# Attention with two heads on halves of the PE array, and full-array gated linear attention, in a transformer kernel

## The chip, the cores and the metric

The kernel runs on one core of one Trainium2 chip. The metric is the device time of one execution in microseconds (us); of several runs the median is given. TensorE (PE) is a 128x128 array: a stationary operand of K rows and M columns is loaded into it (a weight load, PEld), and a moving operand of N columns streams past. The other engines are VectorE (DVE), ScalarE (ACT), GpSimd (POOL) and SyncE (SP, which issues most transfers).

## The reference, cut to what matters

Two blocks of two layers each, batch 1, 256 latent tokens (and 256 context tokens in the first block), width 1024, all in f32. The change touches the attention of the first block's layers and the second block's last mixer. The other stages (adaptive norms, gated feed-forwards, a convolution over tokens, a state-space and mLSTM mixer, convolutional feed-forwards) are unchanged.

```python
def gqa_attention(q, k, v):                    # 6 query heads of 64, 2 key heads
    s = jnp.einsum('bqhgd,bkhd->bhgqk', qi, k).astype(jnp.float32) * scale
    p = jax.nn.softmax(s, axis=-1).astype(v.dtype)
    return jnp.einsum('bhgqk,bkhd->bqhgd', p, v)
...
# neighbourhood_attention: 6 heads; biased scores on the window, plain ones on the context
    p = jax.nn.softmax(s, axis=-1).astype(v.dtype)
    return (jnp.einsum('bhqrj,brqjhd->bqhd', p_win, vw)
            + jnp.einsum('bhqk,bkhd->bqhd', p[..., n_win:], v_ctx))
...
def _gla_scan(q, k, v, la):                    # 4 heads, key 128, value 256, chunks of 64
    bc = jnp.cumsum(la, axis=2)                # la = log_sigmoid(g_lr @ gate_w2 + gate_b) / 16
    b_end = bc[:, :, -1:]
    q_in = q * jnp.exp(bc)
    att = jnp.einsum('bclhk,bcshk->bhcls', q_in, k * jnp.exp(-bc))
    att = jnp.where(_lower_tri(l), att, 0.0)
    o = jnp.einsum('bhcls,bcshv->bclhv', att, v)
    u = jnp.einsum('bclhk,bclhv->cbhkv', k * jnp.exp(b_end - bc), v)
    # states: s_prev[c+1] = exp(b_end[c]) * s_prev[c] + u[c]
    o = o + jnp.einsum('bclhk,cbhkv->bclhv', q_in, s_prev)
```

The scan runs forward and backward over the tokens, and both results are added.

## The kernel before, in words

**Weights.** All weights stream from memory in blocks of 128x1024. SP fetches a block (`raw`), ACT copies it in the rounded type fp32r (`hi`, L115), DVE subtracts (`lo`, L116), and each weight product is three fp32r matmuls, hi·hi, hi·lo and lo·hi (`mm3` L173 to L175, `mm3t` L180 to L182). `W.to(n)` splits blocks ahead of their use. Products of f32 operands (scores times values, transposes, everything in the gated linear attention but its projections) go through the PE as plain f32; one such matmul shows as two passes in the trace, a transpose as one.

**Order.** `Builder.run` calls the stages one after the other: feed-forwards and attention of layer 0 (trace: attention about 480 to 610 us), those of layer 1 (1465 to 1578 us), the second block's mixers and feed-forwards. The gated linear attention (GLA, `mixer1`) stands at about 2256 to 2372 us. A tile framework decides the order of instructions on each engine from priorities and buffers; the kernel's generators (`fill`, `more`) only interleave independent work by hand.

**Attention (`attn`).** Keys of two heads share a 128-partition tile, 64 partitions each, keys or queries in rows and tokens in columns. There are six pairs of heads `j`; for each pair the loop goes over `nt` query tiles `t` of 128 tokens: four in layer 0 and two in layer 1 (only the latent tokens are wanted there). Tiles 0 and 1 (latent) see 512 keys, tiles 2 and 3 (context) 256. Step `i` of `6*nt + DEEP` (L914) does `scores` of its tile, and `values` of the tile two steps earlier (`DEEP` is 2). Between them `fill(n)` puts in pieces of other projections (tiles `pj`), and when those are used up, in the last layer, splits of the feed-forward's first weight blocks.

**Scores (L692).** Per head: the query's hi and lo parts lie on top of each other in the two row halves, so one matmul over K=128 against the doubled key's hi part gives two of the three products, and a second one against the key's lo part, with zeros in the other half, gives the third (L701, L702). A step has four matmuls. Then DVE adds the bias and takes the maximum, and ACT makes the exponentials `P` and their sums `sm`.

**Values (L712).** `P` is transposed on the PE in 128x128 pieces (L720), copied out of PSUM (`PT`, DVE or ACT), and each piece is the stationary operand for 64 columns of values (L729). DVE divides by the sums, and when a pair of heads is finished, its output `ot` is transposed back (`pf`, L910).

**GLA (`mixer1`).** For each of four heads and two directions (h, d): gate logits `lg` from 16 rows (L1446), cumulated and exponentiated on DVE, ACT and POOL (`gates`); then `pairs` transposes the decayed key (`kdT`, L1485) and makes the in-chunk scores `ga` (L1490). `states` multiplies 64 tokens' keys and values (`U`, L1507, K=64, rows 0 to 63 or 64 to 127 by the chunk). `outs` accumulates `go`: the in-chunk part over the whole array (L1521), then each chunk's state into 64 output columns (L1525), on the left or right half of the array by the chunk.

Of the kernel before, what the change touches and what calls it, by code (L numbers as in the profile page):

```python
# [6 lines left out]
F32 = mybir.dt.float32  # L7
# [43 lines left out]
for _name, _w in (("gf", 128), ("gbk", 128), ("rs", 256), ("w2", 512)):  # L51
    GCST[_name] = (_n, _w)
    _n += _w
# [13 lines left out]
class Weights:  # L67
# [24 lines left out]
    def _split(self, urgent=True):  # L92
        nc = self.B.nc
        b = self.split_at
        if b < self.nb:
# [3 lines left out]
            with self.B.tc.high_priority() if urgent and b >= self.B.EARLY else self.B.after_norms():  # L99
# [5 lines left out]
                for o in range(0, TPB * 128, w):  # L105
# [6 lines left out]
                    if aside and self.alone:  # L112
                        nc.gpsimd.tensor_tensor(out=hi, in0=ri, in1=self.B.zero.to_broadcast([128, w]), op=ALU.add)
                    else:
                        nc.scalar.activation(out=hi, in_=ri, func=ACTF.Copy)  # L115
                    eng.tensor_tensor(out=lo, in0=ri, in1=hi.bitcast(F32), op=ALU.subtract)  # L116
# [29 lines left out]
class Builder:  # L146
# [545 lines left out]
    def scores(self, pool, q, kz, t, bias):  # L692

        nc = self.nc
        nk, k0 = (512, 0) if t < 2 else (256, 256)
        Ps = []
        sm = self.sml.tile([128, 2], F32, tag="smx", bufs=6, name="smx")
# [12 lines left out]
        return Ps, sm, nk // 128, k0 // 128  # L710

    def values(self, pool, r, vt, vc, o):  # L712

        nc = self.nc
        r, sm, n, k0 = r
        PT = []
        for P in r:
            pt = self.psmall("pt")
            for kt in range(n):
                nc.tensor.transpose(pt[:, kt * 128:(kt + 1) * 128], P[:, kt * 128:(kt + 1) * 128], self.ident)  # L720
            x = pool.tile([128, 512], F32, tag="ck", name="PT")
            self.evac(x[:, :n * 128], pt[:, :n * 128])
            PT.append(x)
        nc.vector.reciprocal(sm, sm)
        yield
        po = self.psmall("pv")
        for a, x in enumerate(PT):
            for kt in range(n):
                nc.tensor.matmul(po[:, a * 64:a * 64 + 64], x[:, kt * 128:(kt + 1) * 128],  # L729
                                 vt[k0 + kt][:, vc + a * 64:vc + a * 64 + 64], start=kt == 0, stop=kt == n - 1)  # L730
        two = lambda x: x.rearrange("p (a b) -> p a b", a=2)
        self.tt(two(o), two(po[:, :128]), sm.unsqueeze(2).to_broadcast([128, 2, 64]), ALU.mult)

    def attn(self, l, last, end, nxt=None):
# [4 lines left out]
        if l == 0:  # L739
# [3 lines left out]

        kz = [[pool.tile([128, 512], F32R, tag="ck", name="kz") for a in range(4)]
              for i in range(3)]
        for k in kz:
            for a in range(2):
                nc.gpsimd.memset(k[2 + a][64 - 64 * a:128 - 64 * a, :].bitcast(F32), 0.0)

        def keys(k, x):  # L750
            for a in range(2):
                r, o = slice(64 * a, 64 * a + 64), slice(64 - 64 * a, 128 - 64 * a)
                self.act(k[a][r, :], x[r, :])
                self.cp(k[a][o, :], x[r, :])
                self.tt(k[2 + a][r, :], x[r, :], k[a][r, :].bitcast(F32), ALU.subtract)

        def queries(x, scale=1.0):

            q = []
            for a in range(2):  # L760
                y = pool.tile([128, 512], F32R, tag="ck", name="qs")
                r, o = slice(64 * a, 64 * a + 64), slice(64 - 64 * a, 128 - 64 * a)
                self.act(y[r, :Tq], x[r, :Tq], scale=scale)
# [1121 lines left out]
```

## Time and profile before

| | |
|---|---|
| median of 3 runs | 2582.48 us (2582.29 to 2583.18) |
| the profiled execution | 2585.52 us, of which the span of its instructions is 2583.70 us |
| PE busy | 2525.9 us, 98% of the span |
| DVE, ACT, POOL busy | 1731.0, 1193.1, 64.2 us |
| mean granted PE clock | 0.991 of full speed |
| DMA | 375.53 MB, mean 145 GB/s |

The page of the profile gives one profiled execution. A matmul's listed duration includes its way through the array, and matmuls overlap; so the price of one in a stream is the distance between the starts of neighbours, not its duration. "Waits" list the time an engine sat idle and what ended it. The granted clock is 1.00 for TensorE's upper level (2.4 GHz) and 0.50 for its lower one (1.2 GHz).

### The profile page before, as it was taken

Reading aid. Unit: us, or ns where it says so; the run is one execution under the profiler, and the core shown is the slowest. Engines: PE = TensorE matmul, PEld = TensorE weight load, DVE = VectorE, ACT = ScalarE, POOL = GpSimd, SP = SyncE. Lnnn points to the kernel's source line nnn. Section 1 sums busy time; section 2 is a strip of 40 time slices with the busy share of each in tenths; the row PEclk is TensorE's granted clock in tenths of the full one; section 3 lists DMA queues with packets and bytes.
Section 4 is the critical chain, followed back from the end, with each engine's and each line's share of the span. In section 5 each row is a group of like instructions: output and inputs, shape, how many; then the busy total and the mean of one; then the engine's idle time right before and its main releaser. Section 6 shows DMA issues by size and latency. Waiting matters only on the chain.

```text
span 2583.7 us, 37057 instructions
## 1 busy us (share of the span) xinstructions
PE 2525.9 (98%) x13876; PEld 2133.8 (83%) x13876; DVE 1731.0 (67%) x3521; ACT 1193.1 (46%) x2116; POOL 64.2 (2%) x68
## 2 busy tenths in 40 slices
PE   7999999999999999999999999999999999999999
PEld 4888888888888887888888887997988799777997
DVE  4999435665899324899324666556777787666884
ACT  4322234545422223322324555446768566566664
POOL 0000000000000000000000000000030000020000
PEclk9999999999999999999999999999999999999999
DMA  7666231212466222565222323554443355534454
GB/s 274 202 216 222 103 130 62 74 48 74 145 219 216 90 98 98 179 221 196 90 91 89 119 70 118 187 191 157 156 139 131 112 182 182 184 116 139 156 186 156
DMA packets 125028, 375.53 MB, mean 145 GB/s; under 512 B 13872, under 2 KB 15536, under 8 KB 124848
## 3 DMA queue, kind: packets, MB, share of 16 engines
q1 hardware_dynamic: 123840, 370.73, 42.3%
q8 instruction: 109, 1.79, 0.3%
q10 hardware_dynamic: 1008, 2.43, 0.3%
q14 instruction: 71, 0.58, 0.1%
HBM read 372.05 MB, written 1.05 MB: 144 GB/s over the span
## 4 chain that ended last, share of the span: by engine, by line
PE 91%; DVE 3%; ACT 3%; DMA 2%; issue 1%; POOL 0%; SPq 0%; DVEq 0%; ACTq 0%; POOLq 0%
PE pj L173 16%; PE pj L175 15%; PE pj L174 15%; PE po L180 8%; PE po L181 8%; PE po L182 8%; PE pv L729 2%; PE tm L180 2%; PE tm L182 2%; PE tm L181 2%; DMA raw<-in_w 1%; PE gp L173 1%; PE gp L174 1%; PE gp L175 1%; DVE w L116 1%; PE tr L339 1%
## 5 line engine op out<-in xcount | busy, mean ns | idle before, releaser
L115 ACT ACTIVATE w<-raw 128x1024 fp32r<-128x1024 f32 (+1 forms) x588 | 588.8, 1009 | 1002.4 <-PE pj L174 349.4
L116 DVE TENSOR_TENSOR w<-raw,w 128x1024 fp32r<-128x1024 f32 (+1 forms) x588 | 682.0, 1167 | 474.2 <-ACT w L115 470.3
L173 PE MATMUL pj<-uh,w 128*128 128x512 f32 (+1 forms) x1176 | 457.0, 389 | 2.4 <-ACT P L191 2.4
L175 PE MATMUL pj<-uh,w 128*128 128x512 f32 (+1 forms) x1176 | 455.0, 387 | 0.0
L174 PE MATMUL pj<-ul,w 128*128 128x512 f32 (+1 forms) x1176 | 454.9, 387 | 0.0
L614 DVE SCALAR_TENSOR_TENSOR aj<-adaw,cB 128x512 f32<-128x512 f32 x512 | 352.8, 689 | 8.8 <-DMA adaw<-in_wada 0.3
L173 PE MATMUL pj<-u,w 128*128 128x256 f32 x1200 | 341.5, 285 | 0.0
L175 PE MATMUL pj<-u,w 128*128 128x256 f32 x1200 | 340.0, 283 | 0.0
L174 PE MATMUL pj<-u,w 128*128 128x256 f32 x1200 | 339.8, 283 | 0.0
L180 PE MATMUL po<-w,sh 128*128 128x512 f32 x704 | 277.9, 395 | 0.0
L182 PE MATMUL po<-w,sl 128*128 128x512 f32 x704 | 276.9, 393 | 0.0
L181 PE MATMUL po<-w,sh 128*128 128x512 f32 x704 | 276.4, 393 | 0.0
L173 PEld LDWEIGHTS pj<-uh,w 128*128 128x128 f32 x1176 | 221.7, 189 | 50.9 <-ACT P L191 2.8
L175 PEld LDWEIGHTS pj<-uh,w 128*128 128x128 f32 x1176 | 221.6, 188 | 49.4 <-DVE w L116 0.3
L174 PEld LDWEIGHTS pj<-ul,w 128*128 128x128 f32 x1176 | 221.7, 189 | 47.8
L173 PEld LDWEIGHTS pj<-u,w 128*128 128x128 f32 x1200 | 229.4, 191 | 1.8 <-issue 1.3
L175 PEld LDWEIGHTS pj<-u,w 128*128 128x128 f32 x1200 | 229.7, 191 | 0.4 <-issue 0.3
L174 PEld LDWEIGHTS pj<-u,w 128*128 128x128 f32 x1200 | 229.7, 191 | 0.2
L182 PEld LDWEIGHTS po<-w,sl 128*128 128x128 f32 x704 | 132.3, 188 | 30.1
L180 PEld LDWEIGHTS po<-w,sh 128*128 128x128 f32 x704 | 132.3, 188 | 30.0 <-DVE yg L194 0.6
L181 PEld LDWEIGHTS po<-w,sh 128*128 128x128 f32 x704 | 132.3, 188 | 29.2
L194 DVE TENSOR_TENSOR sg<-sg,pj 128x512 f32<-128x512 f32 (+1 forms) x82 | 50.9, 620 | 59.1 <-PE pj L175 58.9
(380 smaller groups left out, 3588.5 us busy)
## 6 DMA issues: line engine op xcount, KB each, us to landing
raw<-in_w SPq DMA_DIRECT2D x554, 512.0 KB, 3.3
adaw<-in_wada SPq DMA_DIRECT2D x288, 256.0 KB, 3.1
bt<-in_bias SPq DMA_DIRECT2D x12, 192.0 KB, 2.4
hl<-in_x ACTq DMA_DIRECT2D x1, 512.0 KB, 5.7
hl<-in_x SPq DMA_DIRECT2D x1, 512.0 KB, 6.6
hc<-in_x SPq DMA_DIRECT2D x1, 512.0 KB, 8.6
hc<-in_x ACTq DMA_DIRECT2D x1, 512.0 KB, 8.9
gc<-in_gcst ACTq DMA_DIRECT2D x1, 512.0 KB, 3.7
```

What stands on the lines that cost most here:

```text
L115: nc.scalar.activation(out=hi, in_=ri, func=ACTF.Copy)
L116: eng.tensor_tensor(out=lo, in0=ri, in1=hi.bitcast(F32), op=ALU.subtract)
L173: mm(ps, w[0], x[0], start=first, stop=False)
L174: mm(ps, w[0], x[1], start=False, stop=False)
L175: return mm(ps, w[1], x[0], start=False, stop=last)
L180: mm(ps, x[0], w[0], start=first, stop=False)
L181: mm(ps, x[0], w[1], start=False, stop=False)
L182: mm(ps, x[1], w[0], start=False, stop=last)
L194: return self.nc.vector.tensor_tensor(out=out, in0=a, in1=b, op=op)
L339: nc.tensor.transpose(p[:, t * 128:(t + 1) * 128], hn[t][c // 4][:, (c % 4) * 128:(c % 4 + 1) * 128], self.ident)
L614: nc.vector.scalar_tensor_tensor(out=x, in0=w, scalar=1.0, in1=self.cB[:, s, i * 512:(i + 1) * 512], op0=ALU.mult, op1=ALU.mult, accum_out ...
L729: nc.tensor.matmul(po[:, a * 64:a * 64 + 64], x[:, kt * 128:(kt + 1) * 128], vt[k0 + kt][:, vc + a * 64:vc + a * 64 + 64], start=kt == 0, ...
```

## The change

**Scores.** The query and the key are each split once into hi and lo tiles of 128x512 (both heads in one instruction on ACT and one on DVE), and a step has six matmuls of K=64: three products, each for head 0 on rows 0 to 63 and head 1 on rows 64 to 127. The doubled tiles, their zeros (POOL) and the half-height copies are gone.

**Values.** Two query tiles (a pair of steps) are finished together. `P` is transposed as before, grouped by key block, always into 512-wide copies `PT`. Values are now stationary (64 columns, head 0 in columns 0 to 63 of the array, head 1 in 64 to 127), and `PT` of both tiles moves (256 columns); the output comes out with features in rows, so the transposes `pf` are gone. The inverse sums are spread by DVE to 128x256 (`rb`), transposed on the PE (2 per pair of tiles), copied by ACT, and multiplied in. A values generator yields twice, and `finish` runs once for two steps.

**Around them.** The table of exponentials is loaded ahead of the loop by a one-element activation on the last query tile. In the last layer, `fill` also runs with n=4 in the two steps behind the last scores (0 before), and from then on the copies `PT` are issued behind the newest weight split (`behind`).

**GLA.** All three small matmuls use the whole array: `lg` multiplies all rows with a table padded with zeros (2 KB wider rows of constants, 768 KB instead of 512 KB), `U` and the state part of `go` take operands padded with zeros (`kz`, `qz`; 16 memsets on POOL, and per (h, d) one ACT and one DVE copy of 64x256 and two ACT copies of 128x128 in place of one copy of 128x256). `pr_qk(3)` moves ahead of the first `pairs`.

```diff
-    def scores(self, pool, q, kz, t, bias):
+    def scores(self, pool, q, kz, t, bias, sm):
...
-        for a in range(2):
-            ps = self.psum("sc")
-            o = slice(t * 128, (t + 1) * 128)
-            nc.tensor.matmul(ps[:, :nk], q[a][:, o], kz[a][:, k0:], start=True, stop=False)
-            nc.tensor.matmul(ps[:, :nk], q[a][:, o], kz[2 + a][:, k0:], start=False, stop=True)
+        for n, (x, y) in enumerate(((0, 0), (0, 1), (1, 0))):
+            for a in range(2):
+                r = slice(64 * a, 64 * a + 64)
+                nc.tensor.matmul(pss[a][:, :nk], q[x][r, o], kz[y][r, k0:], start=n == 0, stop=n == 2)
...
+    def values(self, pool, Ps, sm, vt, vc, k0, out, behind=()):
...
+        for a in range(2):
+            for kt in range(0, n, 2):
+                pt = self.psmall("pt")
+                for k in range(2):
+                    for t in range(2):
+                        o = k * 256 + t * 128
+                        nc.tensor.transpose(pt[:, o:o + 128], Ps[t][a][:, (kt + k) * 128:(kt + k + 1) * 128],
+                                            self.ident)
+                x = pool.tile([128, 512], F32, tag="ck", name="PT")
+                with ExitStack() as es:
+                    for y in behind() if behind else ():
+                        es.enter_context(self.tc.issue_after(y.ins))
+                    self.evac(x, pt)
+                PT.append(x)
+            if a == 0:
+                r = pool.tile([128, 512], F32, tag="ck", name="rb")
+                nc.vector.reciprocal(sm, sm)
+                self.cp(r[:, :256].rearrange("p (t a n) -> p t a n", t=2, a=2), sm.unsqueeze(3).to_broadcast([128, 2, 2, 64]))
+                yield
+
+        p = self.psmall("rb")
+        for t in range(2):
+            nc.tensor.transpose(p[:, t * 128:(t + 1) * 128], r[:, t * 128:(t + 1) * 128], self.ident)
+        self.act(r[:, 256:], p[:, :256])
         yield
         po = self.psmall("pv")
...
+        for kt in range(n):
+            for a in range(2):
+                nc.tensor.matmul(po[a * 64:a * 64 + 64, :256], vt[k0 + kt][:, vc + a * 64:vc + a * 64 + 64],
+                                 PT[(a * n + kt) // 2][:, kt % 2 * 256:kt % 2 * 256 + 256], start=kt == 0,
+                                 stop=kt == n - 1)
+        self.tt(out, po[:, :256], r[:, 256:], ALU.mult)
...
+        self.preload(ACTF.Exp, qk[3][2][:, 0:1])
...
-            n = self.FILL[i * 24 // (6 * nt)] * 4 // nt if i < 6 * nt else 0
+            n = self.FILL[i * 24 // (6 * nt)] * 4 // nt if i < 6 * nt else 4 if last else 0
...
-                nc.tensor.matmul(p[:, :256], self.gcst("w2")[32 * d:32 * d + 16, h * 128:(h + 1) * 128],
-                                 lr[32 * d:32 * d + 16, :], start=True, stop=True)
+                nc.tensor.matmul(p[:, :256], self.gcst("w2")[:, (d * 4 + h) * 128:(d * 4 + h + 1) * 128], lr,
+                                 start=True, stop=True)
...
-                kd[h, d] = pool.tile([128, 256], F32, tag="kd", bufs=8, name="kd")
-                self.evac(kd[h, d], p[:, :256])
+                for a in range(2):
+                    r = slice(64 * a, 64 * a + 64)
+                    (self.act, self.cp)[a](kz[n4(h, d)][r, a].rearrange("p t k -> p (t k)"), p[r, :256])
+                for a in range(2):
+                    o = slice(64 * a, 64 * a + 64)
+                    self.act(qz[n4(h, d)][:, a, :, o], qi[h, d].rearrange("p (t l) -> p t l", t=2)[:, :, o])
...
-                        nc.tensor.matmul(p[:, :256], kd[h, d][r0:r0 + 64, (c // 2) * 128:(c // 2 + 1) * 128],
-                                         vv[c // 2][r0:r0 + 64, h * 256:(h + 1) * 256], start=True, stop=True)
+                        nc.tensor.matmul(p[:, :256], kz[n4(h, d)][:, c % 2, c // 2],
+                                         vv[c // 2][:, h * 256:(h + 1) * 256], start=True, stop=True)
...
-                        nc.tensor.matmul(p[r0:r0 + 64, :256], qi[h, d][:, c * 64:(c + 1) * 64], st[h, d, c],
-                                         start=False, stop=all(x[1] != c for x in todo[n + 1:]))
+                        nc.tensor.matmul(p[:, :256], qz[n4(h, d)][:, c % 2, t], st[h, d, c],
+                                         start=False, stop=n == len(todo) - 1)
...
             pr_qk(2)
+            pr_qk(3)
             for d in range(2):
                 pairs(0, d, *g[0, d])
                 g[1, d] = gates(1, d)
-            pr_qk(3)
```

**What moves on the engines.** Lines of the changed kernel stand one or a few higher than before (L173 is L174, L191 is L192). In the rows below a name is a tile, `<-` its operands, then the moving shape (partitions x columns), and xN a run of equal rows. First the PE in the middle of layer 1's loop, before: values of one step, the transposes back, and the scores of the next step.

```order
L175 MATMUL pj<-uh,w 128x256
L173 MATMUL pj<-uh,w 128x256
L174 MATMUL pj<-ul,w 128x256
L175 MATMUL pj<-uh,w 128x256
L729 MATMUL pv<-vt,PT 128x64 x8
L910 MATMUL pf<-cst,ot 128x128
L701 MATMUL sc<-kz,qs 128x512
L702 MATMUL sc<-kz,qs 128x512
L910 MATMUL pf<-cst,ot 128x128
L701 MATMUL sc<-kz,qs 128x512
L702 MATMUL sc<-kz,qs 128x512
```

The same place of the changed kernel: values of a pair of steps (eight matmuls, on column halves), the six scores on row halves, then projections.

```order
L175 MATMUL pj<-ul,w 128x256
L176 MATMUL pj<-uh,w 128x256
L749 MATMUL pv<-PT,vt 64x256 x8
L704 MATMUL sc<-kzh,qsh 128x512 x2
L704 MATMUL sc<-kzl,qsh 128x512 x2
L704 MATMUL sc<-kzh,qsl 128x512 x2
L174 MATMUL pj<-uh,w 128x256
L175 MATMUL pj<-ul,w 128x256
```

The eight rows of values serve two tiles of queries instead of one, and scores come in three pairs. The other step of a pair has no values but the transposes of the inverse sums:

```order
L175 MATMUL pj<-ul,w 128x256
L176 MATMUL pj<-uh,w 128x256
L727 MATMUL pt<-cst,P 128x128 x8
L743 MATMUL rb<-cst,rb 128x128 x2
L704 MATMUL sc<-kzh,qsh 128x512 x2
L704 MATMUL sc<-kzl,qsh 128x512 x2
L704 MATMUL sc<-kzh,qsl 128x512 x2
```

So the array now goes from its full use (projections, transposes) to column halves, to row halves, and back. Next the ACT at the end of layer 1's attention, before: exponentials, splits of weights (`w<-raw`) and copies of the last transposes.

```order
L191 ACTIVATE PT<-pt 128x512
L115 ACTIVATE w<-raw 128x512 x2
L191 ACTIVATE P,smx<-sc,mx 128x512 x2
L115 ACTIVATE w<-raw 128x512
L191 ACT_TABLE_LOAD
L191 ACTIVATE pl<-smx,eps 128x1
L115 ACTIVATE w<-raw 128x512
L191 ACTIVATE PT<-pt 128x512
L115 ACTIVATE w<-raw 128x512 x2
L191 ACTIVATE o<-pf 128x256
L191 ACTIVATE PT<-pt 128x512 x2
L115 ACTIVATE w<-raw 128x1024
```

And changed:

```order
L115 ACTIVATE w<-raw 128x512
L192 ACT_TABLE_LOAD
L192 ACTIVATE pl<-smx,eps 128x1
L115 ACTIVATE w<-raw 128x512 x3
L192 ACTIVATE o<-ot 128x256
L115 ACTIVATE w<-raw 128x512 x4
L192 ACTIVATE PT<-pt 128x512
L115 ACTIVATE w<-raw 128x1024
L192 ACTIVATE PT<-pt 128x512
L192 ACTIVATE rb<-rb 128x256
L115 ACTIVATE w<-raw 128x1024
L192 ACTIVATE PT<-pt 128x512
```

The last copies `PT` now come after eight split pieces of weights, with two more pieces and the copy of the inverse sums between them. Last the PE in GLA, where keys of the first head are transposed, before:

```order
L175 MATMUL pj<-u,w 128x256
L1485 MATMUL kdT<-cst,t_21440 128x128 x2
L1490 MATMUL ga<-qi,t_21437 128x128 x2
L173 MATMUL pj<-u,w 128x256
L174 MATMUL pj<-u,w 128x256
L175 MATMUL pj<-u,w 128x256
```

Changed:

```order
L176 MATMUL pj<-u,w 128x256
L1497 MATMUL kdT<-cst,t_21296 128x128 x2
L1506 MATMUL ga<-qi,t_21293 128x128 x2
L1497 MATMUL kdT<-cst,t_21309 128x128 x2
L181 MATMUL tm<-w,u 128x512
L182 MATMUL tm<-w,u 128x512
L1506 MATMUL ga<-qi,t_21306 128x128 x2
L183 MATMUL tm<-w,u 128x512
```

The projections of the last head (48 rows `pj`), which stood between and behind the first two `kdT`, are done ahead of them, and `tm` products (values' projection) follow instead.

## Rows read from the trace of the kernel before

**Rows 1.** Parts 1 and 4 of the page, whole span.
```profile
PE 2525.9 (98%) x13876; PEld 2133.8 (83%) x13876; DVE 1731.0 (67%) x3521; ACT 1193.1 (46%) x2116; POOL 64.2 (2%) x68
...
PE 91%; DVE 3%; ACT 3%; DMA 2%; issue 1%; POOL 0%; SPq 0%; DVEq 0%; ACTq 0%; POOLq 0%
```

**Rows 2.** Groups by line and form on PE, both attentions (480 to 1570).
```profile
L729 PE MATMUL pv<-vt,PT 128*128 128x64 f32 x480 | 59.8, 274 | 0.0
L701 PE MATMUL sc<-kz,qs 128*128 128x512 f32 x48 | 20.6, 437 | 4.2 <-DVE kz L209 2.6 <-DVE qs L200 1.4
L701 PE MATMUL sc<-kz,qs 128*128 128x256 f32 x24 | 7.4, 323 | 1.2 <-ACT P L191 1.2
```

**Rows 3.** Timeline of PE in layer 1: start, duration, engine, line, count.
```profile
1508.20 0.39 PE L702 MATMUL sc<-kz,qs 128*128 128x512 f32 x1
1508.43 0.40 PE L701 MATMUL sc<-kz,qs 128*128 128x512 f32 x1
...
1508.89 0.28 PE L173 MATMUL pj<-uh,w 128*128 128x256 f32 x1
1509.01 0.27 PE L174 MATMUL pj<-ul,w 128*128 128x256 f32 x1
...
1547.74 1.89 PE L729 MATMUL pv<-vt,PT 128*128 128x64 f32 x16
1549.47 1.04 PE L720 MATMUL pt<-cst,P 128*128 128x128 f32 x8
```

**Rows 4.** Timeline of PE in the GLA mixer: one U among full-array matmuls.
```profile
2353.56 0.40 PE L180 MATMUL po<-w,mxh 128*128 128x512 f32 x1
2353.88 0.70 PE L1507 MATMUL U<-vv,kd 64*128 64x256 f32 x2
2354.51 0.50 PE L181 MATMUL po<-w,mxh 128*128 128x512 f32 x1
2354.84 0.40 PE L182 MATMUL po<-w,mxl 128*128 128x512 f32 x1
```

**Rows 5.** Timeline of PE in the GLA mixer: two U together.
```profile
2299.37 0.70 PE L1507 MATMUL U<-vv,kd 64*128 64x256 f32 x4
2300.00 0.50 PE L182 MATMUL tm<-w,u 128*128 128x512 f32 x1
```

**Rows 6.** Timeline of PE in the GLA mixer: go on column halves.
```profile
2362.72 1.08 PE L1525 MATMUL go<-st,qi 128*64 128x256 f32 x6
2363.73 0.50 PE L182 MATMUL po<-w,mxl 128*128 128x512 f32 x1
```

**Rows 7.** Waits of PE in layer 1 (1465 to 1578): total, times, longest.
```profile
PE pj L173 <- ACT P L191: 2.4, 1, 2.4
```

**Rows 8.** Busy time by stretch: PE, PEld, DVE, ACT, POOL, granted clock, DMA share, GB/s.
```profile
500.00:600.00 100.00, 97.50 (x629) 86.09 (x628) 62.25 (x142) 49.31 (x128) 0.00 (x0) 0.98 0.14 47
596.40:599.80 3.40, 3.40 (x17) 3.21 (x16) 1.70 (x6) 0.70 (x3) 0.00 (x0) 0.50 0.00 0
2262.10:2272.40 10.30, 10.30 (x33) 7.59 (x33) 5.50 (x13) 5.95 (x11) 0.00 (x0) 0.50 0.13 49
2272.40:2288.00 15.60, 14.51 (x87) 12.81 (x85) 14.62 (x23) 11.37 (x23) 2.11 (x3) 1.00 0.40 139
```

**Rows 9.** Timeline of PE at the start of the GLA mixer.
```profile
2259.55 2.36 PE L1446 MATMUL lg<-lr,gc 16*128 16x256 f32 x10
```

**Rows 10.** Waits of PE in the GLA mixer (2256 to 2372).
```profile
PE kdT L1485 <- DVE t L194: 3.0, 3, 1.4
```

**Rows 11.** Groups of ACT in the GLA mixer (busy, mean ns, idle before).
```profile
L191 ACT ACTIVATE kd<-kdT 128x256 f32<-128x256 f32 x8 | 2.9, 379 | 0.4 <-PE kdT L1485 0.4
```

**Rows 12.** Timeline of ACT at the end of layer 1's attention.
```profile
1559.21 1.08 ACT L191 ACTIVATE PT<-pt 128x512 f32<-128x512 f32 x2
1560.17 1.07 ACT L115 ACTIVATE w<-raw 128x1024 fp32r<-128x1024 f32 x1
```

More of the change, by code (lines that the diff above doesn't have):

```diff
@@ L50 @@
 _n = 0
-for _name, _w in (("gf", 128), ("gbk", 128), ("rs", 256), ("w2", 512)):
+for _name, _w in (("gf", 128), ("gbk", 128), ("rs", 256), ("w2", 1024)):
     GCST[_name] = (_n, _w)
@@ L709, in scores @@
             Ps.append(P)
-        return Ps, sm, nk // 128, k0 // 128
-    def values(self, pool, r, vt, vc, o):
+        return Ps
+    def values(self, pool, Ps, sm, vt, vc, k0, out, behind=()):
         nc = self.nc
-        r, sm, n, k0 = r
+        n = 4 - k0
         PT = []
[L717 to L724, printed above, removed]
+        for a in range(2):
[21 more added lines that the diff above has]
+        self.act(r[:, 256:], p[:, :256])
@@ L725, in values @@
         yield
         po = self.psmall("pv")
[L727 to L732, printed above, removed]
+        for kt in range(n):
[3 more added lines that the diff above has]
+                                 stop=kt == n - 1)
@@ L742, in attn, with keys @@
         self.ts(g8, self.v("qkg", 2 * l), 0.125, None, ALU.mult)
[L744 to L755, printed above, removed]
-        def queries(x, scale=1.0):
[L759 to L763, printed above, removed]
-                self.stt(y[o, :Tq], x[r, :Tq], scale, y[r, :Tq].bitcast(F32), ALU.mult, ALU.subtract)
-                q.append(y)
-            return q
+        def keys(x):
+            return self.split(pool, x, 512, "ck", "kz")
+        def queries(x, scale=1.0):
+            y = self.parts(pool, 512, "ck", "qs")
+            self.scaled(y, x, scale, slice(0, Tq))
+            return y
+        ks = [None] * 3
         gps, u = self.group(self.pre1(pool, l, 1, 512, 2), 3, 512, True)
         for j in range(2):
-            keys(kz[1 + j], gps[1 + j])
+            ks[1 + j] = keys(gps[1 + j])
         vt = []
@@ L801, in second @@
                 p = yield from half(512)
-                keys(kz[1], p)
-            heads[j] = q, kz[1 + j % 2], bt
+                ks[1] = keys(p)
+            heads[j] = q, ks[1 + j % 2], bt
             if j == 2:
@@ L883, in rotate @@
             if j == 0:
-                keys(kz[0], x)
+                ks[0] = keys(x)
             else:
@@ L901, in attn, with finish @@
         rotate(3)
+        self.preload(ACTF.Exp, qk[3][2][:, 0:1])
         oh = []
-        def finish(step, r):
-            j, t, vc, o = step
-            yield from self.values(pool, r, vt, vc, o[:, t * 128:(t + 1) * 128])
-            if t == nt - 1:
-                pf = self.psmall("pf")
-                for i in range(nt):
-                    nc.tensor.transpose(pf[:, i * 128:(i + 1) * 128], o[:, i * 128:(i + 1) * 128], self.ident)
-                oh.append(self.split(pool, pf[:, :Tq], Tq, "ck", "o"))
+        def finish(j, t, vc, o, Ps, sm):
+            yield from self.values(pool, Ps, sm, vt, vc, 2 if t else 0, o[:, t * 128:t * 128 + 256], (lambda: self.W.latest) if ahead else None)
+            if t == nt - 2:
+                oh.append(self.split(pool, o[:, :Tq], Tq, "ck", "o"))
         before = []
@@ L939, in attn @@
                 self.ada(1)
-            if i >= self.DEEP:
+            if i >= self.DEEP and i % 2 == 0:
                 f = before.pop(0)
                 next(f)
-                fill(n - n // 2)
+            fill(n - n // 2)
+            if i >= self.DEEP:
                 next(f, None)
-            else:
-                fill(n - n // 2)
         fill(99)
```

40 lines of the change are left out of this document (26 added, 14 removed).

## The prediction

> **What bounds the kernel now.** I read the page first: PE is busy 2525.9 us of 2583.70, and it is 91% of the chain that ended last [rows 1]. So a microsecond of the PE stream is worth about a microsecond of time, and other engines count only where the PE waits for them. Then the groups of PE instructions in the two attentions [rows 2] for counts, the timeline of the PE there and in GLA [rows 3 to 6] for the distances between starts, which are the prices, the waits of the PE [rows 2, 7, 10], and the busy time of stretches with their granted clock [rows 8].
>
> **Values.** Before, there are 480 passes of 64 columns [rows 2]. Sixteen of them take from 1547.74 to 1549.47, so 0.108 us each [rows 3], 51.9 us in all. After, values are made for pairs of tiles: per pair of heads one over four key blocks (512 keys) and one over two in layer 0, and one over four in layer 1. Each block is two heads of two passes of 256 columns, so 12 pairs of tiles have 16 passes and 6 have 8: 240 passes, in two column halves. What does such a pass cost? A lone U (two passes of 256 columns) takes from 2353.88 to 2354.51, 0.63 us [rows 4]. Of that 0.19 is the change into another use of the array (next paragraph), which leaves 0.22 a pass. Do halves run together? Six passes of `go` on column halves, two on one side and four on the other, take 1.01 us [rows 6]: four passes of 0.22 and 0.13 for the change; one after the other they would need 1.45. So I count 120 slots of 0.22, 26.4 us, and gain 25.5. The transposes back (36) are replaced by as many transposes of inverse sums: nothing.
>
> **Scores.** L701 and L702 each have 48 matmuls of 512 columns and 24 of 256 [rows 2], so 24 steps of four and 12 of four. The distances are 0.23 and 0.12 [rows 3]. After, six per step on row halves. Two U in opposite row halves (four passes) take 0.63 us [rows 5], as long as one alone [rows 4]; these are plain f32, and an fp32r matmul on half the rows is nowhere in this trace. Bounds: three slots a step (halves together) or six (one after the other). I take three, by the nearest row. Gain: 24 x 0.23 + 12 x 0.12 = 7.0 us.
>
> **Changes in the use of the array.** Before the U, a full 512-column matmul takes 0.32 us to the next start where 0.23 is usual; after it the first full one takes 0.33 [rows 4]. So a change costs 0.09 for the array to run empty and about 0.10 for a weight load that nothing covers; into column halves, with 64 columns to load, 0.13 by `go`. The attentions have none of these changes now. In the changed kernel's order I count 108: 41 into row halves, 20 into column halves, 47 back to the whole. Cost 41 x 0.19 + 20 x 0.13 + 47 x 0.19 = 19.3 us. This is what eats most of the gain: the PE stream of the attentions gets 25.5 + 7.0 - 19.3 = 13.2 us shorter. Lower bound of the price: 0.09 each (every load hidden), 9.7 us; upper: two loads show instead of one, 0.29, 31 us. I take the value that the rows of such changes have.
>
> The Trainium skill (TensorE: Matmul & The Clock Gate, Part 3, The mechanism) has a rule against this change: weight loads overlap with running matmuls only when their row groups differ. Two heads on column halves share all rows, so by it each slot of values would show its load. The rows disagree so far: four slots of `go` keep to 0.22. The price if it held is rival C.
>
> **Waits and clock of the attentions.** The PE waits 5.4 us in front of scores for keys, queries and `P` (4.2 + 1.2) [rows 2] and 2.4 us behind an exponential [rows 7]. The keys' and queries' chains are shortened from two copies, two casts and two subtractions to one and one of full height, and the table load goes ahead of the loop. I give back 4.2 of 7.8. At 596.4 the clock stands at 0.50 for 3.40 us [rows 8], behind such waits; two more stretches in layer 1 are like it. Each costs half its length, 5.1 in all; I give back 3.3, since other waits may remain. Against it, new waits. The inverse sums go DVE, PE, ACT, DVE before `ot` is ready, but at least one fill stands between, and only the last pair is exposed. There `behind` holds the last `PT` (0.54 us) on ACT until a split of 1.07 us is through [rows 12], and the values of the last pair on the PE wait for it, with five products in front of them at 0.23: 1.5 us. A pair's first `P` waits for the second, so two steps' `PT` come at once and take the same PSUM buffers: 1.5 us more. Together -4.2 - 3.3 + 3 = -4.5. What hides the rest (60 copies `PT` of 512 columns in place of 48 of 512 and 24 of 256, the spread sums): DVE is busy 62 and ACT 49 of 100 us in layer 0's loop [rows 8]; where DVE were full, the copies of `rb` (18 of about 0.4 us) would cost up to 7 us. POOL's zeros for keys go away, off the path.
>
> **GLA.** Three parts. (1) About 35 changes of use, 0.19 each, disappear: -6.7. In return `go` has six slots instead of four in eight groups, 16 x 0.22 = +3.5, and of the 48 passes of U some seven that ran beside another one stand alone, +1.5: net -1.7. (2) From 2262.1 the clock is at 0.50 for 10.30 us with PE busy throughout [rows 8], after ten passes of `lg` that use 16 rows [rows 9]: 5.15 us lost. With full rows the fall may not come; no row shows a full-height `lg`, so gains from 0 to 5.15 are possible. I take 4, since the rest of the stream around it (full-height matmuls) keeps 1.00. (3) The PE waits 3.0 us in three places for `kdT`'s operand [rows 10]. The 48 matmuls of `pr_qk(3)`, 5.7 us at 0.12, now stand in front of the first one, but the second `kdT` loses its cover, so I take 1.3. Sum -7.0. The extra work is 8 x (one ACT of 64x256 at about 0.38, the nearest row [rows 11], one such DVE, two ACT of half the size) for one 0.38 copy: about 5 us of ACT and 3 of DVE. DVE is the tight one, 14.62 of 15.60 us before `kdT` [rows 8], but the copies come behind `kdT`, beside `tm` matmuls; if that cover fails U waits for `kz`, up to 4 us. The constants' longer transfer has the projections of GLA in front of its first reader; the 16 zeros on POOL find it idle (2.11 of 15.60).
>
> **Sum.** -13.2 - 4.5 - 7.0 = -24.7 us. The profiled execution takes 2585.52 (its span 2583.70 and 1.8 around it), 3.0 more than the median of the runs; it would become 2560.8, and the median 2582.48 - 24.7 = 2557.8. I forecast 2558, with a range of its own from 2547 to 2569: the price of a change weighs most (10 down, 12 up), the values, waits and GLA have 2 to 4 each, and they don't all err one way.
>
> **Rivals.**
> A. Row halves of fp32r don't run together: six slots a step, so 24 x 3 x 0.23 + 12 x 3 x 0.12 = 20.9 us back, -3.8, time 2578.7. For it: no such pair in the trace. Against: U's pairs. A tenth.
> B. Handoffs eat half: PE waits for `PT`, `rb` or `kz` because two tiles' copies come at once, and a wait of some us brings another 3.4 us stretch at half clock. At 18 pairs, 0.5 us each is 9 us, plus two such stretches 3.4: -12.3, time 2570. For it: the scores' waits stand at just these places now. Against: DVE and ACT have a third of their time free. 14%.
> C. Weight loads are not hidden between matmuls on the same rows, the mechanism of the Trainium skill's rule above: half of 0.10, for 64 columns, in each of 120 slots is 6, and 0.10 in the two further slots of 36 score steps is 7.2: 13.2 back, time 2571. Against: `go`'s slots of 0.22. 5%.
> D. Slower: each score matmul on half the rows stands alone and shows its load, as the first one behind a change does (0.33 for 512 columns, 0.22 for 256). A step then costs 1.98 or 1.32 instead of 0.92 or 0.48: 24 x 1.06 + 12 x 0.84 = 35.5 us more where I count 7.0 less; with the rest kept the sum is -24.7 + 42.5 = +17.8, time 2600. It decides from about 24.7 us of loss, 0.7 us per step. Speaks for it: one U's second pass does follow its first by 0.32 behind a change. Against: within a run of U that extra is gone. 4%.
> E. The clock in GLA does not come back and `kdT` waits as before: +5.3, time 2563, inside the range.
>
> **How the numbers follow.** The forecast with E has 67%, A 10, B 14, C 5, D 4. The two-sided 80% range takes B and C in and leaves out A and D and the tail below: 2545 to 2575. What a measurement of this kernel can tell from no change is about 0.2%, 5.2 us. Faster by more: all of the forecast, B, C and a little under half of A, 0.90; within 0.2%: most of A, 0.05; slower: D and a part of A with B, 0.05.
>
> **What the changed profile would show.** `pv` as 240 passes in pairs whose starts are 0.22 apart, a four-block group in about 1.9 us. Scores of 512 columns in three pairs, about 0.9 us with both changes. Between a projection and the first score 0.32, behind it 0.33. No half clock at 2262; no `U` or `go` with 64 rows or columns. PE's busy time near 2500 us. I would be wrong if the six scores stand 0.23 apart one by one (A, D), if PE's waits for `PT`, `rb` or `kz` exceed some 10 us (B), or if a change costs clearly more than 0.19 in a direction not seen before, from columns straight to rows.

## The result and the profile after

The changed kernel takes 2555.93 us in the median of four runs (2553.72 to 2557.38), the kernel before 2582.83 in the runs beside it. The ratio is 0.9894, with a 95% interval from 0.9882 to 0.9907: 26.9 us less, where 24.7 was forecast. The page after, parts 1 and 4 [rows 1]:

```profile
PE 2502.3 (98%) x13708; PEld 2092.9 (82%) x13708; DVE 1710.8 (67%) x3471; ACT 1189.9 (47%) x2124; POOL 63.3 (2%) x72
...
PE 90%; DVE 4%; ACT 3%; DMA 2%; issue 1%; POOL 0%; SPq 0%; DVEq 0%; ACTq 0%; POOLq 0%
```

PE has 23.6 us less to do in a span 30.4 us shorter, so some 7 us of idle PE went too. The groups by line and form on PE in both attentions of the changed kernel (busy, mean ns, idle before), which answer to [rows 2]:

```profile
L727 PE MATMUL pt<-cst,P 128*128 128x128 f32 x240 | 33.6, 276 | 1.0 <-ACT PT L192 1.0
L749 PE MATMUL pv<-PT,vt 128*64 128x256 f32 x240 | 31.3, 387 | 0.0
L704 PE MATMUL sc<-kzh,qsh 64*128 64x512 f32 x48 | 12.4, 496 | 0.0
...
L743 PE MATMUL rb<-cst,rb 128*128 128x128 f32 x36 | 7.1, 280 | 0.0
L704 PE MATMUL sc<-kzh,qsh 64*128 64x256 f32 x24 | 5.3, 378 | 0.7 <-ACT P L192 0.6
```

Values are 240 passes instead of 480, and in front of all scores the PE waits 0.7 us where it waited 5.4. The timeline of the PE in layer 1 shows the prices:

```profile
1478.84 0.29 PE L176 MATMUL pj<-uh,w 128*128 128x256 f32 x1
1479.06 1.95 PE L749 MATMUL pv<-PT,vt 128*64 128x256 f32 x16
1480.94 0.51 PE L704 MATMUL sc<-kzh,qsh 64*128 64x512 f32 x2
1481.27 0.40 PE L704 MATMUL sc<-kzl,qsh 64*128 64x512 f32 x2
1481.51 0.40 PE L704 MATMUL sc<-kzh,qsl 64*128 64x512 f32 x2
1481.84 0.39 PE L174 MATMUL pj<-uh,w 128*128 128x256 f32 x1
```

Sixteen passes of values take 1.88 us, eight slots of 0.216 and 0.15 for one change in the use of the array. Six scores take 0.90 us: the `x2` rows are two heads that start together, three slots of 0.23 and 0.20 for a change. Last the projection in front of the values: 0.22 to the next start where 0.12 is usual. These are the forecast's prices.

The busy time by stretch in layer 0's loop, where the half clock of [rows 8] stood, in layer 1's loop, and in GLA:

```profile
488.00:588.00 100.00, 99.31 (x604) 70.24 (x603) 64.63 (x131) 56.24 (x139) 1.67 (x1) 1.00 0.16 52
1455.00:1550.00 95.00, 93.51 (x609) 71.71 (x609) 70.08 (x136) 59.95 (x129) 4.01 (x4) 1.00 0.35 116
2228.00:2245.00 17.00, 16.98 (x86) 14.22 (x84) 12.87 (x25) 15.27 (x27) 1.67 (x2) 1.00 0.35 121
2310.00:2318.90 8.90, 6.81 (x33) 5.50 (x32) 5.94 (x8) 7.11 (x11) 0.00 (x0) 1.00 0.58 198
2318.90:2322.30 3.40, 3.40 (x10) 2.61 (x9) 3.02 (x4) 2.38 (x5) 0.00 (x0) 0.50 0.56 196
```

No stretch of the attentions is below 1.00. At the start of GLA, where 10.30 us were at 0.50, the clock is up too; but later in GLA the PE is idle for 2.1 us of 8.9 and then runs 3.40 us at 0.50.

To see where time went I counted the products with streamed weights (`pj`, `po`, `gp`, `tm`) on the PE. There are 11,688 in each kernel, in nearly the same order, so the distance between the starts of the same two is the length of a stage. In us, each from one profiled execution:

```
kernel       layer 0    layer 1    GLA        all other
             1950-2400  5850-6450  9900-10500 stages
before       174.07     166.63     177.96     2036.57
after        161.98     146.18     177.96     2037.76
attn_only    162.07     146.18     178.65     2035.30
gla_only     172.73     166.17     177.97     2036.13
old_scores   162.32     148.21     181.25     2036.92
old_values   180.56     155.34     178.16     2036.05
no_ahead     163.53     149.40     181.85     2035.18
ahead_only   172.39     159.61     178.16     2035.41
no_preload   161.97     145.82     177.87     2034.71
lg_full      161.96     146.16     176.31     2039.16
lg_qk        161.98     146.18     177.35     2037.55
u_go_full    161.98     146.19     181.46     2034.80
by_head      162.81     145.85     181.20     2036.54
cum_late     161.97     146.14     180.99     2039.89
```

The two attentions give 12.1 and 20.5 us, GLA nothing. In the last two columns single profiles lie up to 4 us from the kernel before. Stretches at half clock, which stand at other places in every kernel, are a part of that but not all of it: the other stages of cum_late are 3.3 us longer than those of before, with 2 us less at half clock.

### The profile page after: what moved, and what is told of

Same layout as the page of the kernel before. It is cut to its first block, busy times and chain, and to the rows that moved or that the text cites. A ratio compares the mean times of both kernels' runs of the same rounds, so it can differ in the third digit from the quotient of the medians.

```text
span 2553.3 us, 36663 instructions
## 1 busy us (share of the span) xinstructions
PE 2502.3 (98%) x13708; PEld 2092.9 (82%) x13708; DVE 1710.8 (67%) x3471; ACT 1189.9 (47%) x2124; POOL 63.3 (2%) x72
## 4 chain that ended last, share of the span: by engine, by line
PE 90%; DVE 4%; ACT 3%; DMA 2%; issue 1%; POOL 0%; SPq 0%; DVEq 0%; ACTq 0%; POOLq 0%
PE pj L174 16%; PE pj L176 16%; PE pj L175 16%; PE po L181 8%; PE po L182 8%; PE po L183 8%; PE tm L181 2%; PE tm L182 2%; PE tm L183 2%; DMA raw<-in_w 1%; PE gp L174 1%; PE gp L175 1%; PE gp L176 1%; DVE w L116 1%; PE tr L340 1%; PE pv L749 1%
## 5 line engine op out<-in xcount | busy, mean ns | idle before, releaser
L174 PE MATMUL pj<-uh,w 128*128 128x512 f32 (+1 forms) x1176 | 458.3, 390 | 0.4 <-ACT P L192 0.4
L174 PE MATMUL pj<-u,w 128*128 128x256 f32 x1200 | 340.8, 284 | 0.0
L174 PEld LDWEIGHTS pj<-uh,w 128*128 128x128 f32 x1176 | 221.1, 188 | 54.8 <-issue 5.4
L174 PEld LDWEIGHTS pj<-u,w 128*128 128x128 f32 x1200 | 229.0, 191 | 0.6
```

What stands on the lines that cost most here:

```text
L174: mm(ps, w[0], x[0], start=first, stop=False)
```

## Experiments

**Run attn_only: the attention's edits alone.** The edit takes the diff's parts in `w2`, `gcst` and `mixer1` back.

> The attention's edits without those of GLA. By the prediction's sum (attention -17.7, GLA -7.0) the time should be 8 to 9 us above the changed kernel's, about 2565. The rival, read from the changed kernel's trace: the stretch with GLA is as long as before (177.96 us in both), so the GLA edits give nothing, and this kernel takes the changed kernel's time, about 2556, within 2.

Measured: 2552.87 us, ratio 0.9891 (0.9876 to 0.9906). The rival holds: the attention's edits carry all of the gain, 29.4 us against the runs of before beside it, and the forecast had 17.7 for them.

**Run gla_only: GLA's edits alone.**

> GLA's edits without those of the attention. By the sum 2582.5 - 7.0 = 2575.5. The rival: no change, 2582 within 2, with the half clock at the start of GLA gone but as much time lost again later in the same stage (waits, longer U and go).

Measured: 2583.72 us, ratio 1.0008 (0.9999 to 1.0017). No gain; the forecast's -7.0 is refuted, and the rival holds. The busy time of the whole stage before, and the PE's wait at its end for `mxh` (the rounded part of the mixer's output, made by ACT):

```profile
2227.40:2405.40 178.00, 170.72 (x851) 131.22 (x850) 120.05 (x219) 111.62 (x235) 15.78 (x20) 0.97 0.38 127
PE po L180 <- ACT mxh L191: 1.2, 1, 1.2
```

The same in gla_only, with the stretch behind that wait and the waits for `kdT`:

```profile
2225.10:2403.10 178.00, 169.51 (x850) 138.24 (x850) 125.43 (x227) 115.15 (x251) 21.18 (x36) 0.99 0.39 129
2348.40:2351.80 3.40, 3.40 (x10) 2.75 (x9) 2.99 (x4) 2.03 (x4) 0.00 (x0) 0.50 0.53 189
PE po L180 <- ACT mxh L191: 2.1, 1, 2.1
PE kdT L1493 <- DVE t L194: 0.8, 2, 0.5
```

The stage has 10.2 us at half clock before and 3.4 here. That gives the PE 3.4 us back, but its busy time falls by 1.2 only: at full clock it would be some 2.2 us longer than before. Of that, from start to next start, `go` takes 1.5 more and `U` 1.0 less; the rest lies in matmuls beside them. The PE is also idle 1.2 us more. The waits for `kdT` fall from 3.0 to 0.8, but others grow, among them the one for `mxh`. In front of it on ACT stands a load of its table of functions, ahead of the copies `tr` that come before `mxh`:

```profile
2343.06 1.28 ACT L191 ACT_TABLE_LOAD   x1
2344.36 0.60 ACT L191 ACTIVATE tr<-tm 128x512 f32<-128x512 f32 x1
```

All five profiles of kernels with `U` and `go` over the whole array have this load 3.8 us ahead of the first `po` that reads `mxh`, the wait of 2.1 us, and a half clock of 3.4 us soon behind. In the nine others the corresponding load, the one after `rs`, stands 23 us ahead of that `po`, the wait is 1.2 us, and no half clock follows.

**Run old_scores: the scores of before in the changed kernel.**

```diff
-        for n, (x, y) in enumerate(((0, 0), (0, 1), (1, 0))):
...
+            nc.tensor.matmul(ps[:, :nk], q[a][:, o], kz[a][:, k0:], start=True, stop=False)
+            nc.tensor.matmul(ps[:, :nk], q[a][:, o], kz[2 + a][:, k0:], start=False, stop=True)
```

> The changed kernel with the scores of before (four full-array matmuls a step, doubled keys and queries), all else kept. By the prediction's prices the PE stream gets 7.0 us of score slots back to pay and saves the changes into row halves: 36 changes instead of 108, 13 us less, so 6 us shorter; the keys' and queries' longer chains cost 4 us of waits and clock: 2554, slightly below the changed kernel. The rival: it is the short chains of keys and queries that removed the waits and half-clock stretches in layer 1, worth more than the prices of the changes: 2560 or more.

Measured: 2557.59 us, ratio 0.9907 (0.9893 to 0.9920), between the theory and the rival, and not to be told from the changed kernel's 0.9894. The attentions' stages are 0.3 and 2.0 us longer. The waits of the PE in its layer 1 (total, times, longest), and a stretch at half clock in its layer 0:

```profile
PE sc L702 <- DVE qs L201: 1.4, 2, 1.1
PE pj L174 <- ACT P L192: 1.1, 1, 1.1
PE sc L702 <- DVE kz L210: 0.8, 1, 0.8
583.30:590.10 6.80, 6.27 (x25) 4.15 (x24) 5.31 (x15) 4.51 (x12) 0.00 (x0) 0.50 0.00 1
```

Of these 3.3 us the changed kernel has 0.4 left, and it has no half clock there. The PE stream alone is shorter with the old scores: without the PE's idle time and the clock's loss the two stages take 4.1 and 0.5 us less than in the changed kernel, where the prices had said 6 (0.90 + 0.09 + 0.10 = 1.09 for six on row halves among projections, against 0.93 for four). So on row halves the scores cost PE time, and the shorter chains of keys and queries pay for it with less waiting.

**Run old_values: the values of before in the changed kernel.**

```diff
-        def finish(j, t, vc, o, Ps, sm):
-            yield from self.values(pool, Ps, sm, vt, vc, 2 if t else 0, ...)
+        def finish(step, r):
+            yield from self.values(pool, r, vt, vc, o[:, t * 128:(t + 1) * 128])
```

(`values` and the loop's end are those of before)

> The changed kernel with the values of before (P transposed is stationary, 64 columns of values move, one tile per step), scores on row halves kept. By the sum: 25.5 us of values back, 36 changes fewer (5 to 6 us): 2576. The rival, that the values' gain was mostly something else (waits, fewer instructions): below 2568.

Measured: 2578.57 us, ratio 0.9990 (0.9981 to 0.9999). Values alone carry 22.6 us of the 26.9; 20 were expected, and the rival (below 2568) falls. In this kernel's profile the two stages are 27.7 us longer than in the changed one, of which 5.1 are a stretch at half clock of 10.2 us behind layer 0's attention.

**Run no_ahead: attn_only without the splits among the last steps.** In the stage table layer 1 gave more than its PE stream and the waits of [rows 2] and [rows 7] could. In the trace of before, the PE behind the last attention:

```profile
1577.55 0.39 PE L182 MATMUL po<-w,o 128*128 128x512 f32 x1
1582.04 0.52 PE L339 MATMUL tr<-cst,hn 128*128 128x128 f32 x3 [4.11 <-DVE hn L204]
```

and ACT at the same time:

```profile
1572.05 1.06 ACT L115 ACTIVATE w<-raw 128x1024 fp32r<-128x1024 f32 x1 [2.00 <-DMA raw<-in_w]
1574.51 1.16 ACT L115 ACTIVATE w<-raw 128x512 fp32r<-128x512 f32 x2 [1.40 <-DMA raw<-in_w]
1575.57 0.58 ACT L191 ACTIVATE yg<-po 128x512 f32<-128x512 f32 x1
```

In ACT's order, splits of weights that wait for their transfers (2.00 and 1.40 us) stand in front of `yg`, the copy from which the next norm is made, and the norm's transposes come 4.11 us late. The edit:

```diff
-            n = self.FILL[i * 24 // (6 * nt)] * 4 // nt if i < 6 * nt else 4 if last else 0
+            n = self.FILL[i * 24 // (6 * nt)] * 4 // nt if i < 6 * nt else 0
...
-    (lambda: self.W.latest) if ahead else None
+    None
```

> The attention's edits alone (run attn_only), without the weight splits in the two last steps of layer 1 and without the copies' place behind them. In the trace of before the PE stands 4.3 us between the last attention's output projection and the next norm's transposes, and runs 3.4 us at half clock behind it; in attn_only it stands 0.3 us there. Theory: the early splits free ACT and DVE for the norm's chain, so without them the wait and the half clock are back: 2552.9 + 4 + 1.7 = about 2558.5, and the wait can be seen in front of the transposes. Rival (the prediction's): the early splits hold the last copies up and cost 1.5 us, so the time falls to about 2551.

Measured: 2558.45 us, ratio 0.9903 (0.9888 to 0.9918). That is 5.6 us above attn_only in the medians, the theory's number; by the ratios it is 3.1, and the intervals overlap. The timeline of its PE, with the wait in front of the same transposes:

```profile
1553.25 1.82 PE L340 MATMUL tr<-cst,hn 128*128 128x128 f32 x5 [2.49 <-DVE hn L205]
```

Its busy time by stretch, at half clock right behind that wait:

```profile
1553.20:1556.60 3.40, 3.23 (x10) 2.20 (x11) 3.11 (x12) 2.12 (x5) 0.00 (x0) 0.51 0.00 0
```

The wait and the half clock are back, but the wait is 2.5 us and not 4, and layer 1's stage is 3.2 us longer than in attn_only. The rest of the 5.6 isn't found there, so that the theory's sum came out was in part luck.

**Run ahead_only: the splits among the last steps, in the kernel before.** One edit:

```diff
-            n = self.FILL[i * 24 // (6 * nt)] * 4 // nt if i < 6 * nt else 0
+            n = self.FILL[i * 24 // (6 * nt)] * 4 // nt if i < 6 * nt else 4 if last else 0
```

> The kernel before with one edit: weight splits in the two last steps of layer 1's attention. Theory: 4 us of wait and 1.7 us of half clock ahead of the next norm go: 2582.3 - 5.5 = about 2577. Rival: the wait belongs to the old order of values and transposes, not to the splits: within 1.5 us of 2582.

Measured: 2577.56 us, ratio 0.9980 (0.9970 to 0.9990), 4.8 us less. On ACT the copy `yg` now waits for the PE only:

```profile
1565.58 1.15 ACT L115 ACTIVATE w<-raw 128x512 fp32r<-128x512 f32 x2
1566.98 0.60 ACT L191 ACTIVATE yg<-po 128x512 f32<-128x512 f32 x1 [0.24 <-PE po L182]
```

So this part works alone (the interval leaves out no change); layer 1's stage is 7.0 us shorter in the profile. From the other side (no_ahead) it is worth between 3 and 6 us.

**Run no_preload: attn_only without the early table of exponentials.**

```diff
-        self.preload(ACTF.Exp, qk[3][2][:, 0:1])
```

> attn_only without the early load of the table of exponentials. Theory: the 2.4 us wait of the PE for the first exponentials in layer 1, and the half clock behind it (1.7 us), come back: 2556 to 2557. Rival: the shorter key and query chains had removed them: no change, 2553.

Measured: 2552.58 us, ratio 0.9885 (0.9868 to 0.9901): no change. The wait of [rows 7] is 0.3 us without the early load and 0.4 with it, so the load was not its cause. In old_scores, with the early load, it is 1.1: the chains of keys and queries take part in it.

**Run lg_full: attn_only with the gate logits over all rows.**

```diff
-                nc.tensor.matmul(p[:, :256], self.gcst("w2")[32 * d:32 * d + 16, h * 128:(h + 1) * 128],
-                                 lr[32 * d:32 * d + 16, :], start=True, stop=True)
+                nc.tensor.matmul(p[:, :256], self.gcst("w2")[:, (d * 4 + h) * 128:(d * 4 + h + 1) * 128], lr,
+                                 start=True, stop=True)
```

> attn_only with one edit of GLA: the gate logits over all rows; U, go, their operands and the order of the projections as before. Theory: the 10.2 us at half clock at the start of GLA go away and nothing else is lost, 5 us: 2548. Rival: the half clock only moves to a later wait of the same stage, and the gain is 0 to 2 us: 2551 to 2553.

Measured: 2553.05 us, ratio 0.9883 (0.9868 to 0.9898). The half clock at the start of GLA is gone and the time is the same. Busy time by stretch, in attn_only:

```profile
2228.10:2238.30 10.20, 10.20 (x32) 7.48 (x32) 5.89 (x14) 5.58 (x12) 0.00 (x0) 0.50 0.12 44
```

And in lg_full:

```profile
2228.00:2238.00 10.00, 9.98 (x57) 8.48 (x56) 8.38 (x19) 7.60 (x15) 0.00 (x0) 1.00 0.46 160
2253.00:2256.20 3.20, 0.83 (x7) 0.63 (x6) 3.20 (x5) 1.97 (x5) 0.02 (x1) 1.00 0.38 120
2256.20:2259.60 3.40, 2.73 (x13) 2.73 (x14) 2.70 (x5) 2.72 (x9) 1.89 (x2) 0.50 0.68 253
```

With the full clock the PE comes to `kdT` earlier, stands nearly idle there (0.83 us of 3.20, while DVE is busy for all of it) and falls to half clock. The waits of the PE for `kdT` (total, times, longest) in attn_only:

```profile
PE kdT L1489 <- DVE t L195: 3.3, 3, 1.7
```

And in lg_full:

```profile
PE kdT L1489 <- DVE t L195: 3.7, 2, 3.0
```

The stage is 2.3 us shorter in the profile, less than the 5.1 that the clock gave back. The other stages are 3.9 us longer in this profile than in attn_only's, so the time of the whole kernel can't show the 2.3.

**Run lg_qk: lg_full and the last head's projections earlier.**

```diff
             pr_qk(2)
+            pr_qk(3)
...
                 g[1, d] = gates(1, d)
-            pr_qk(3)
```

> attn_only with the gate logits over all rows and with the last head's projections ahead of the first pairs; U, go and their operands as before. In lg_full the PE came to kdT earlier, waited 3.2 us for DVE there, and fell to half clock for 3.4 us. Theory: the moved projections cover that wait, so both go: 3 to 4 us below attn_only, about 2549. Rival: the chain on DVE sets the stage's length whatever the PE does before it; the wait comes back at the next kdT or ga: 2552 to 2553.

Measured: 2553.04 us, ratio 0.9879 (0.9864 to 0.9894). The rival: the first head's `kdT` waits no more, but the second head's waits 2.3 us, and a half clock of 3.4 us stands at 2266.6.

**Run u_go_full: attn_only with U and go over the whole array.**

The changed kernel with the edits of the last two runs undone, so that only `kz`, `qz` and their matmuls are left of GLA's part, with the fewer buffers that the change gives this stage (`qi` 6 instead of 8, `at` 4 instead of 8).

> attn_only with U and go over the whole array and their padded operands; gate logits and order as in attn_only. Theory: fewer changes in the use of the array but more slots for go, and more copies on ACT and DVE in front of U: 0 to 2 us above attn_only, 2553 to 2555. Rival, by the prediction's term: 1.7 us below, 2551.

Measured: 2556.75 us, ratio 0.9895 (0.9880 to 0.9910). No gain, and perhaps a loss, which the interval doesn't separate from none. In its profile GLA is 2.8 us longer than in attn_only, with as much at half clock (10.2 us) in both, and the wait for `mxh` is 2.1 us. The run also qualifies another step of the forecast. It has the 16-row logits as before, and the clock beside them, at 2226.3, stays up; it falls behind the wait for `kdT`. Its busy time by stretch:

```profile
2226.30:2236.50 10.20, 10.04 (x51) 7.52 (x51) 7.13 (x17) 8.23 (x16) 0.00 (x0) 1.00 0.31 106
2251.50:2258.30 6.80, 5.67 (x27) 5.67 (x28) 5.37 (x8) 4.45 (x15) 3.55 (x4) 0.50 0.60 196
```

Of the seven profiles with 16-row logits five have 10.2 us at 0.50 beside them, and two, this one and ahead_only's, have none; of the seven with full rows none has. So full rows go with the full clock there, but what brings the fall with 16 rows stays open.

**Run by_head: the products of a step ordered by head.**

```diff
-        for n, (x, y) in enumerate(((0, 0), (0, 1), (1, 0))):
-            for a in range(2):
+        for a in range(2):
+            for n, (x, y) in enumerate(((0, 0), (0, 1), (1, 0))):
```

> attn_only with the six score matmuls of a step in another order: the three products of head 0, then those of head 1. Matmuls on the same rows follow each other, so only the third and the fourth can run together: five slots instead of three, 24 x 2 x 0.23 + 12 x 2 x 0.12 = 13.9 us more, 2567. If the halves overlap in any order: no change, 2553. If weight loads show between matmuls on the same rows, four more loads of 0.10 a step, 14 us on top: 2581.

Measured: 2555.72 us, ratio 0.9888 (0.9872 to 0.9905). This tests nothing: the scheduler put most pairs together again, as the timeline shows:

```profile
1466.29 0.51 PE L704 MATMUL sc<-kzh,qsh 64*128 64x512 f32 x2
1466.63 0.40 PE L704 MATMUL sc<-kzl,qsh 64*128 64x512 f32 x2
```

**Run cum_late: lg_qk with the first head's gates ahead of the others' scans.**

```diff
             cumulate()
+            scan(0)
...
                 g[0, d] = gates(0, d)
+            scan(1)
...
                 g[1, d] = gates(1, d)
+            scan(2)
+            scan(3)
```

> lg_qk with one more edit: the cumulated gates of the first head and all that its kdT needs on DVE come before those of the other three heads, whose scans (six pairs of DVE instructions, about 5 us, and weight subtractions between them) stood in front of it. Theory: the chain on DVE sets the kdT waits of GLA; then PE's waits for kdT and ga (3.1 us in lg_qk) fall under 1.5 us and the half clock behind them goes, 3 us in the stage. Rival: the wait is given back at the second head's kdT or behind it, and the stage keeps its 177 us.

Measured: 2558.08 us, ratio 0.9893 (0.9875 to 0.9912). The theory falls; the wait is given back as the rival had it, but the stage takes 181.0 us in the profile and not 177. PE's waits between 2228 and 2300 are

```profile
PE kdT L1491 <- DVE t L195: 2.4, 1, 2.4
PE pj L176 <- DVE w L116: 1.1, 3, 0.6
PE U L1513 <- DVE st L201: 1.0, 1, 1.0
PE ga L1496 <- DVE at L195: 0.4, 1, 0.4
```

The wait for `kdT` stays, at the second head as in lg_qk, and weight blocks (`pj`) and states (`U`) come late as well. So it is not one late instruction; whatever is put first on DVE, something else on it is late. That DVE's total work in this stretch sets the length fits lg_full, lg_qk and this run, but I didn't run a kernel with less of that work, so it stays an argument.

No run beats the changed kernel beyond the intervals. attn_only, no_preload, lg_full and lg_qk lie some 3 us below it, which these runs can't tell from nothing.

## Why the prediction was right, and where it was not

**Prices and streams: right.** Values in 120 slots of 0.22, scores in three slots, 0.09 and 0.10 for a change in the use of the array: all three stand in the timeline after. The row halves of fp32r, which no row of before showed, run together; rivals A and D fall with that, and C falls with slots of 0.216 for values whose row group never changes. The rule of the Trainium skill that the prediction took for C (TensorE: Matmul & The Clock Gate, Part 3, The mechanism: loads overlap only when row groups differ) is not borne out by these slots; the same section's text also lets a load run ahead into a background weight buffer, and no run here tests that. The stages of before and attn_only differ by 12.0 and 20.4 us. Taking out the waits (7.8 to 2.0), the norm's wait (4.1 to none) and four half-clock stretches (4 x 1.7), 32.4 - 16.7 = 15.7 us are left for the PE streams, where the sum had 13.2. By the two runs with parts undone it is the values that make this gain, and the scores take some 5 us of it back.

**Waits and clock of the attentions: mis-sized.** The term was -4.5 and measured about -16.7. Three things in it. First, the place behind the attention: I looked at the waits up to 1578, and the 4.1 us for the norm begin there. The term counted the splits among the last steps only as a cost of 1.5 us for the last `PT`; ahead_only shows a gain of 4.8, and no_ahead one of 3 to 6. Second, "I give back 4.2 of 7.8" was 6.8, and all four half clocks went (three counted, 3.3 us credited). Third, of the 3 us of new waits, 1.0 came (`pt` for `PT`; with it the 7.8 are 2.0); rival B, half of the gain lost in handoffs, did not happen. The credit to the early table load was wrong in its cause: no_preload.

**GLA: wrong.** -7.0 was forecast, and gla_only shows a ratio of 1.0008, whose interval (0.9999 to 1.0017) goes from 0.3 us of gain to 4.4 of loss. Against the three terms: "net -1.7" for `U` and `go` was +2.2 in gla_only (+0.9 in u_go_full) by the PE's busy time at full clock, of which the slots of `go` and `U` themselves are only 0.5, and u_go_full's stage is 2.8 us longer than attn_only's. The clock gave 3.4 us back where 4 were credited: the fall at the logits didn't come, but 3.4 us at half clock stand at the end of the mixer, behind the longer wait for `mxh`. And the PE's idle time grew by 1.2 us where 1.3 less were credited, although `kdT` did wait less. Together 2.2 - 3.4 + 1.2 = 0 us. The step that failed is that the new copies on ACT would be hidden beside `tm` matmuls. It was checked for their time and for `U` waiting on `kz` (0.2 us in u_go_full), not for the new order on ACT, which brings a table load of 1.28 us in front of the last copies.

The clock term doesn't stand alone either. In lg_full, without the new `U` and `go`, the clock gives 5.1 us back and the stage keeps 2.3 of them: the PE comes earlier to operands that DVE has not made yet, waits 3.0 us at one place, and a half clock follows. Rival E, priced at +5.3, had GLA's gain right (next to none) but not the way: it expected the clock not to come back and `kdT` to wait as before, and neither was so.

The forecast of 2558 was met within 2.1 us since two errors of opposite sign cancelled: attention 12 us under, GLA 8 to 10 over. That the number was met so closely is luck; the range was right about the whole, the terms were not.

**Open.** The changed kernel is 3 us slower than attn_only in the medians, inside the intervals. In the profiles its GLA stage is 0.7 us shorter and the other stages are 2.5 us longer, so the 3 us aren't seen in GLA. Whether the GLA edits cost that much together isn't settled.

## What to carry to other kernels

Where the PE is the bound, count passes and changes in the use of the array, and price both from neighbouring starts in the trace: that much could be forecast here within 3 us of 13. Then read the waits past the end of the edited stage: work that waits for a transfer (here splits of weights), ahead of a copy on the same engine, delayed the next stage's first step, and putting it earlier paid 4.8 us in the kernel before and 3 to 6 in attn_only. Padding operands to the whole array saves changes in its use but adds passes and copies: here the PE's busy time at full clock grew, and the new order of copies put a table load of ACT in the PE's way. And time at half clock isn't all worth giving back: of 5.1 us in lg_full's GLA stage 2.3 were kept, since the PE then waited for DVE.

## What the hardware showed that was not expected

Two fp32r matmuls of 512 columns on opposite row halves start within 0.01 us of each other and take the time of one (three such pairs in slots of 0.23 us). The granted clock beside the same code differs from kernel to kernel: the same 16-row logits had 10.2 us at 0.50 in attn_only and 1.00 throughout in u_go_full and ahead_only, where the fall came some 25 us later, behind a wait. In the attentions and GLA the lowered stretches looked at stand behind stretches in which the PE was partly idle, but for those at the logits.
